# A four-layer attention decoder: another order of one head's TensorE steps, query and table buffers moved, one logits bank per block

## The chip, the core and the metric

The kernel runs on one core of a Trainium2 chip. The time is device microseconds (us) of one execution. The kernel before takes 1056.14 us, the median of 3 runs (1054.42 to 1060.06). The profiled execution took 1054.78 us; its trace spans 1053.0 us, at a mean granted TensorE clock of 0.992.

## The reference

Four layers work on a sequence of 512 tokens of width 1024. Layer i uses mixer i mod 3: multi-head latent attention (MLA), sliding-window attention (SWA), forgetting attention (FoX), and MLA again. Each has 16 heads with values of 64 columns, and all is in fp32:

```
for i in range(4):
    y = mixer[i % 3](x)                      # (o * silu(gate)) @ w_out
    x = layernorm(8 ** 0.25 * x + y)
# one head o:  s = scale * q @ k.T (+ bias) ; causal mask ; p = softmax(s) ; o = p @ v
# MLA: q and k have 64 plain columns and 32 rotary ones, from low-rank projections with an RMS norm
# SWA: a query sees 128 keys at most; ALiBi bias, a sink per head, 4 key/value heads for 16 query heads
# FoX: bias cum[q] - cum[k], cum = running sum of log_sigmoid(f)
```

## The kernel before, in words

Tensors lie with 128 rows on the partitions. A matrix product in fp32 is made of fp32r products: each operand is split into a high part (a cast on ACT) and a low part (a subtraction on VectorE or GpSimd), and high x high, high x low and low x high are summed in PSUM, so a product takes three passes. The logits of SWA and FoX take two passes, because high and low halves of a 64-column key are stacked in the 128 rows.

**Weights.** One list holds all weight units in the order of their use. A unit is loaded by SP's DMA queue into a raw tile of 512 KB (`_raw`, L254, pool `p_wr`, tag "wr", 3 buffers), cast on ACT (L289), and its low part is subtracted in halves of 512 columns on GpSimd (L293; on VectorE for the output weights "O"). `W()` splits up to three units ahead of the one in use. When the split of unit k is issued, the load of unit k+2 is issued behind it.

**PSUM.** Eight banks: three for projections ("pp", `bank()`), two for logits ("ss"), two for transposes ("pt"), one for a head's output ("oo").

**A head.** Queries come in four blocks of 128. The step S(qb) makes the logits of block qb (TensorE, `mm`, L305), and VectorE adds the bias or mask and takes the row extreme (L844 in MLA, L905 in SWA, L1024 and L1026 in FoX). After the fourth block the softmax tail runs: exponentials on ACT (L420), a reciprocal on VectorE (L426), scaling of blocks 0 to 2 on GpSimd (L431) and of block 3 on ACT (L429). The step T transposes the probabilities through the identity matrix (L479 for MLA and FoX, three groups of 4, 3 and 3 blocks; L926 for SWA, two groups of 4 and 3). Each group fills one "pt" bank, which is emptied by a cast on ACT (L465) and a subtraction on VectorE (L309) into a tile "PT". The step PV multiplies with the values (TensorE), ACT and VectorE empty the bank (L503, L504), and for every second head GpSimd multiplies with the gate (L511).

**Order on TensorE.** In the loop over heads the order of TensorE's instructions is the program order (a manual schedule); the other engines' orders are planned by a scheduler. The steps of iteration h come from `slots`:

```
sn = st["s_fn"](h + 1, st) if h + 1 < H else []
pv = [lambda: self.attn_pv(h - 1, st)] if h else []
return sn[:2] + pv + sn[2:] + st["t_fn"](h, st)
```

That is S0 S1 of head h+1, PV of head h-1, S2 S3 of head h+1, and all transposes of head h (T0 T1 T2, or T0 T1 in SWA). Between the steps `heads` spreads filler: the projections of later heads. `PAIRS` lists for each pair of heads which ones: K, Q, V and G are key, query, value and gate projections, R the rotary query projection for four heads. The last pair is filled with steps of the output projection (`out_part`, 49 steps of three matmuls, L305, named "po" or "pp"), `TAIL` and `EXTRA` of them; `finish` makes the rest and the layer norm after a hand-written list (`FINISH`: f is so many output steps, k, m the closing ones, r the residual on VectorE, L545, s, t, a, b the norm), in which VectorE's order is the program's too.

**MLA's start.** `PRO` gives how many gate and value steps (g and d) are put between the transposes of the compressed queries, the rotary projection, the query projection and the key projection. Behind the key projection and nine further gate steps the head loop begins, and the remaining value steps fill its first blocks.

**Rotary part of MLA's queries.** The projection R ends in a bank; VectorE multiplies it with a table of cosines and sines (L811), which a DMA brings from memory (L808, input "cs", 512 KB) into a tile of pool `p_rt`, tag "tq". The product stays in that tile, ACT casts it and GpSimd subtracts (L813, L814) into "rq", and for each head two DMAs (L831, 128 KB each) copy its rows into the query tile of that head, pool `p_qk`, tag "qk", which holds the plain part (ACT L825, VectorE L826).

## Time and profile before

| | us |
|---|---|
| median of 3 runs (lowest, highest) | 1056.14 (1054.42, 1060.06) |
| profiled execution, its span | 1054.78, 1053.0 |
| PE busy (5416 matmuls) | 993.0 (94% of the span) |
| ACT, VectorE (DVE), GpSimd (POOL) busy | 623.0, 610.3, 508.8 |
| head loops of layers 0, 1, 2, 3 | 61.4 to 240.9, 307.9 to 454.8, 546.0 to 755.4, 835.1 to 1013.0 |

The four head loops together take 713.7 us of the span; the rest is the layers' projections ahead of the loops, the ends of the output projections and the layer norms. In the page of the profile a busy share is a mean over the span. In the rows further down a row of a wait reads: engine, output tile and line of the waiting instruction, then engine, tile and line of what ended the wait, then the idle time in us, the number of waits and the longest. A row of the order of instructions reads: start in us, duration in us, engine, line, operation, output from input, partitions x elements, count, and in brackets the idle time ahead of it with what ended it. A row of windows reads: window, its length, then busy time and count of each engine, the granted clock (1.00 is full), the DMA share and the GB/s. "SPq" is SP's DMA queue.

### The profile page before, as it was taken

Reading aid. Unit: us, or ns where it says so; the run is one execution under the profiler, and the core shown is the slowest. Engines: PE = TensorE matmul, PEld = TensorE weight load, DVE = VectorE, ACT = ScalarE, POOL = GpSimd, SP = SyncE. Lnnn points to the kernel's source line nnn. Section 1 sums busy time; section 2 is a strip of 40 time slices with the busy share of each in tenths; the row PEclk is TensorE's granted clock in tenths of the full one; section 3 lists DMA queues with packets and bytes.
Section 4 is the critical chain, followed back from the end, with each engine's and each line's share of the span. In section 5 each row is a group of like instructions: output and inputs, shape, how many; then the busy total and the mean of one; then the engine's idle time right before and its main releaser. Section 6 shows DMA issues by size and latency. Waiting matters only on the chain.

```text
span 1053.0 us, 15941 instructions
## 1 busy us (share of the span) xinstructions
PE 993.0 (94%) x5416; PEld 843.7 (80%) x5416; DVE 610.3 (58%) x1501; ACT 623.0 (59%) x1350; POOL 508.8 (48%) x572
## 2 busy tenths in 40 slices
PE   8999898999999999999999999999999998999895
PEld 8978787778888887788988888887879787777784
DVE  2566666853735656819334555566366567567717
ACT  4477877753346777723456666666344588677712
POOL 5755555333245664413456666642175556553303
PEclk9999999999999999999999999999999999999998
DMA  6452322452542122414342343335252533223412
GB/s 222 133 152 93 91 69 80 126 170 77 204 120 81 61 81 81 147 56 160 106 145 82 108 113 101 110 119 167 74 164 74 178 103 90 74 71 101 130 41 81
DMA packets 37218, 116.77 MB, mean 111 GB/s; under 512 B 5376, under 2 KB 5632, under 8 KB 36880
## 3 DMA queue, kind: packets, MB, share of 16 engines
q1 hardware_dynamic: 37136, 115.75, 35.7%
q8 instruction: 43, 0.70, 0.3%
q14 instruction: 39, 0.32, 0.1%
HBM read 92.62 MB, written 8.42 MB: 96 GB/s over the span
## 4 chain that ended last, share of the span: by engine, by line
PE 43%; ACT 3%; DVE 3%; issue 2%; DMA 1%; POOL 1%; SPq 0%; DVEq 0%; POOLq 0%; ACTq 0%
PE pp L305 29%; PE ss L305 4%; PE po L305 4%; PE oo L305 3%; PE ptt L479 3%; DMA wr<-in_w 1%; ACT w L289 1%; ACT P L420 1%; POOL r L609 1%; PE pxt L356 1%; DVE PT L309 1%; DVE r L593 0%; ACT PT L465 0%; DVE w L293 0%; DMA q<-rq 0%
## 5 line engine op out<-in xcount | busy, mean ns | idle before, releaser
L305 PE MATMUL pp<-xT,w 128*128 128x512 f32 (+1 forms) x1440 | 376.9, 394 | 0.0
L293 POOL TENSOR_TENSOR w<-wr,w 128x512 fp32r<-128x512 f32 x202 | 241.8, 1222 | 204.9 <-ACT w L289 125.5
L305 PEld LDWEIGHTS pp<-xT,w 128*128 128x128 f32 x1440 | 249.3, 190 | 36.9
L431 POOL TENSOR_TENSOR P<-P,rs 128x256 f32<-128x256 f32 (+2 forms) x192 | 113.3, 618 | 130.7 <-DVE rs L426 129.7
L420 ACT ACTIVATE P<-P,m 128x256 f32<-128x256 f32 (+3 forms) x256 | 137.7, 539 | 63.9 <-DVE m L844 32.6
L289 ACT CAST w<-wr 128x1024 fp32r<-128x1024 f32 (+4 forms) x117 | 115.3, 990 | 101.3 <-PE pp L305 47.1
L309 DVE TENSOR_TENSOR PT<-ptt,PT 128x384 fp32r<-128x384 f32 (+1 forms) x176 | 104.1, 601 | 65.5 <-ACT PT L465 65.2
L305 PE MATMUL pp<-w,xT 128*128 128x256 f32 (+2 forms) x768 | 112.8, 300 | 2.3 <-ACT xT L360 1.9
L305 PEld LDWEIGHTS pp<-w,xT 128*128 128x128 f32 x768 | 105.4, 191 | 3.8 <-ACT xT L360 2.4
L465 ACT CAST PT<-ptt 128x384 fp32r<-128x384 f32 (+1 forms) x176 | 88.3, 513 | 26.9 <-PE ptt L479 21.6
L479 PE MATMUL ptt<-ident,P 128*128 128x128 f32 x480 | 77.1, 275 | 23.6 <-DVE PT L309 21.6
L479 PEld LDWEIGHTS ptt<-ident,P 128*128 128x128 f32 x480 | 58.5, 140 | 49.7 <-DVE PT L309 32.9
L305 PEld LDWEIGHTS oo<-PT,v 128*128 128x128 f32 x512 | 81.8, 188 | 12.6 <-DVE PT L309 2.9
L305 PE MATMUL pp<-cT,w 128*128 128x512 f32 x312 | 90.3, 404 | 0.0
L305 PE MATMUL ss<-kt,q 128*128 128x128 f32 (+3 forms) x384 | 82.6, 323 | 6.5 <-ACT kt L797 2.7
L305 PE MATMUL oo<-PT,v 128*128 128x256 f32 (+3 forms) x512 | 85.7, 307 | 1.4 <-DVE PT L309 1.4
L504 DVE TENSOR_TENSOR o<-oo,o 64x512 f32<-64x512 f32 x64 | 44.0, 688 | 68.0 <-ACT o L503 67.7
L305 PEld LDWEIGHTS ss<-kt,q 128*128 128x128 f32 x384 | 65.2, 188 | 19.8 <-ACT kt L797 3.6
L305 PE MATMUL pp<-w,oT 128*128 128x512 f32 x288 | 79.3, 402 | 0.0
L844 DVE CUSTOM_DVE_ANT_0 P<-ss,mask 128x128 f32<-128x128 f32 (+3 forms) x128 | 61.6, 487 | 23.8 <-PE ss L305 21.5
L305 PE MATMUL po<-wo,oT 128*128 128x512 f32 x288 | 70.7, 395 | 0.0
L511 POOL TENSOR_TENSOR o<-o,g 128x512 f32<-128x512 f32 x28 | 36.3, 1295 | 61.8 <-DVE o L504 61.8
(120 smaller groups left out, 1433.2 us busy)
## 6 DMA issues: line engine op xcount, KB each, us to landing
wr<-in_w SPq DMA_DIRECT2D x110, 512.0 KB, 3.4
q<-rq SPq DMA_DIRECT2D x64, 128.0 KB, 2.4
xd<-r SPq DMA_DIRECT2D x12, 512.0 KB, 2.9
r<-xd SPq DMA_DIRECT2D x12, 512.0 KB, 3.9
wr<-in_w SPq DMA_DIRECT2D x16, 336.0 KB, 3.4
kd<-kd SPq DMA_DIRECT2D x20, 256.0 KB, 4.3
tq<-in_cs SPq DMA_DIRECT2D x8, 512.0 KB, 3.9
cb<-cd SPq DMA_DIRECT2D x16, 256.0 KB, 3.4
```

What stands on the lines that cost most here:

```text
L289: nc.scalar.copy(w[0][:, :c], r[:, :c])
L293: eng.tensor_tensor(w[1][:, a:b], r[:, a:b], w[0][:, a:b].bitcast(F32), op=ALU.subtract)
L305: self.nc.tensor.matmul(out, l, r, start=start, stop=stop)
L309: (eng or self.nc.vector).tensor_tensor(out, src, hi.bitcast(F32), op=ALU.subtract)
L356: nc.tensor.transpose(v, xt[:, c:c + 128], self.ident[:])
L420: nc.scalar.activation(v, v, AF.Exp, bias=m[:, c:c + 1], scale=-1.0, accum_out=sums[:, c:c + 1])
L431: nc.gpsimd.tensor_tensor(v, v, rs[:, c:c + 1].to_broadcast([128, v.shape[1]]), op=ALU.mult)
L465: nc.scalar.copy(pt[:, 0, :n], ps[:, :n])
L479: nc.tensor.transpose(ps[:, c:c + 128], Ps[qb][:, kb * 128:(kb + 1) * 128], self.ident[:])
L504: nc.vector.tensor_tensor(o[a, :], o_ps[a, :], o[a, :], op=ALU.add)
L511: eng.tensor_tensor(o[:], o[:], g[:], op=ALU.mult)
L844: nc.vector.tensor_tensor_reduce(out=P[:, :n], in0=ps[:, :n], in1=self.mask[:, S - n:], scale=1.0, scalar=3e38, op0=ALU.add, op1=ALU.min, ...
```

## The change

The step order of an iteration is new (`iteration`). Per head of MLA and FoX it is now: T0 of head h, S2 of head h+1, T1, S3 of head h+1, T2, then S0 and S1 of head h+2, then PV of head h itself. S0 and S1 of a head are thus issued one iteration earlier than before, PV of a head right in its own iteration. In SWA (two transposes) it is S2 S3 of head h+1, T0 T1, S0 S1 of head h+2, PV; round the loop these are the same neighbours as before. `GROUPS` takes the place of `PAIRS` and `EXTRA`: the same projections are dealt to groups of iterations counted in a rotation fitting the new order, "+n" stands for n output steps, and the first group (count 0) holds head 0's four logits, S0 and S1 of head 1 and the remaining value steps. `TAIL` has fewer entries, one for each step of the last two iterations.

The third query buffer: for heads with h mod 3 = 2 the query tile comes from pool `p_rt`, tag "tq", the buffer in which the table was before. The table's tile now comes from pool `p_wr`, tag "wr", the three raw-weight buffers.

In SWA each of the four logits blocks gets an "ss" bank tile of its own, where two blocks shared one.

In the last layer `FINISH` takes 16 free output steps instead of 22 ahead of the closing ones (the "+7" and the new tail hold another number too), and `PRO` puts four value steps beside the key projection in both MLA layers, where it had two and none.

No product is added or left out.

```diff
@@ -40,16 +40,16 @@
     'f91 k0 f99 k1 r0 s0 k2 m1 r1 t0 s1 r2 s2 k3 m4 a0 b0 x0 h3 t2 t1 a1 b1 m3 i3 s3 x1 a2 b2 t3 a3 x2 b3 x3',
     'f38 k0 f99 k1 k3 r0 s0 r1 t0 k2 s1 a0 b0 a1 h3 t1 m3 x0 r2 b1 m5 s2 i3 s3 a2 t2 b2 x1 t3 a3 b3 x2 x3',
     'f33 k3 f99 k0 k1 r0 s0 r1 t0 m4 a0 k2 s1 b0 t1 a1 x0 b1 m4 r2 h3 s2 a2 x1 t2 i3 b2 s3 t3 a3 b3 x2 x3',
-    'f22 k0 k1 k2 f99 r0 r1 s0 s1 t0 m1 z0 k3 r2 t1 s2 a1 m5 b1 m2 t2 h3 a2 b2 i3 s3 a3 t3 b3',
+    'f16 k0 k1 k2 f99 r0 r1 s0 s1 t0 m1 z0 k3 r2 t1 s2 a1 m5 b1 m2 t2 h3 a2 b2 i3 s3 a3 t3 b3',
 )
-PRO = ((2, 1, 2, 2), (2, 1, 19, 0))
+PRO = ((2, 1, 2, 4), (2, 1, 19, 4))
 PRE = 4
 
 TAIL = (
-    (1, 1, 1, 1, 1, 1, 2, 3, 4, 1, 2, 3),
-    (1, 1, 1, 1, 2, 2, 4, 4, 1, 4),
-    (1, 1, 1, 1, 1, 1, 3, 4, 4, 1, 2, 3),
-    (1, 1, 1, 1, 1, 1, 2, 3, 4, 1, 2, 3),
+    (1, 1, 1, 2, 3, 4, 1, 2, 4),
+    (1, 2, 2, 3, 4, 2, 4),
+    (1, 1, 1, 2, 3, 4, 1, 2, 4),
+    (1, 1, 1, 2, 3, 4, 1, 2, 4),
 )
 
 
@@ -63,14 +63,14 @@
 
 
 
-PAIRS = (
-    ("K1 Q1 R1 G2", "K2 Q2 V1", "K3 Q3 R2 G3", "K4 Q4 G4", "K5 Q5 R3 G5", "K6 Q6 G6", "K7 Q7 G7"),
-    ("G0 Q2", "G1 Q3", "G2 Q4", "G3 Q5", "G4 Q6", "G5 Q7", "G6 G7"),
-    ("V2 Q2 K2", "G2 Q3 K3", "G3 Q4 K4", "V3 Q5 K5", "G4 Q6 K6", "G5 Q7 K7", "G6 G7"),
+
+GROUPS = (
+    ((0, "K1 Q1"), (1, "V1"), (2, "R1 K2 Q2 G2"), (2, "K3 Q3 G3"), (2, "R2 K4 Q4 G4"), (2, "K5 Q5 G5"), (2, "R3 K6 Q6 G6"),
+     (2, "K7 Q7 G7"), (1, "+7")),
+    ((0, "G0"), (2, "Q2 G1"), (2, "Q3 G2"), (2, "Q4 G3"), (2, "Q5 G4"), (2, "Q6 G5"), (2, "Q7 G6"), (2, "G7 +8")),
+    ((0, "G2"), (2, "V2 Q2 K2"), (2, "G3 Q3 K3"), (2, "G4 Q4 K4"), (2, "V3 Q5 K5"), (2, "G5 Q6 K6"), (2, "G6 Q7 K7"), (2, "G7 +16")),
 )
-STREAM = tuple(jobs(" ".join(k)) for k in PAIRS)
-
-EXTRA = (3, 0, 8, 3)
+STREAM = tuple(tuple(j for _, k in g for j in jobs(k) if j[0] != "+") for g in GROUPS)
 FIRST = (jobs("G0 G1 K0 R0 Q0 V0"), jobs("Q0 Q1"), jobs("K0 Q0 G0 K1 Q1 G1"))
 
 def layer_units(kind):
@@ -610,54 +610,62 @@
         nc.sync.dma_start(self.t["out"][tb * 128:(tb + 1) * 128, :], r[:])
 
 
-    def job_cols(self, kind, n, a):
-
+    def job(self, layer, st, make, n, a):
+
+        kind = layer % 3
+        if n == "+":
+            return islice(st["order"], a), a * 3 * 512
         if kind == 0 and n in "KQR":
-            return (6 if n == "K" else 9) * 512
-        return 96 * 256 if n == "V" and kind else 24 * 512
-
-    def slots(self, layer, st, h):
-
-        sn = st["s_fn"](h + 1, st) if h + 1 < H else []
-        pv = [lambda: self.attn_pv(h - 1, st)] if h else []
-        return sn[:2] + pv + sn[2:] + st["t_fn"](h, st)
-
-    def run_heads(self, layer, st, make, pre=iter(()), npre=3):
+            return make[n](a), (6 if n == "K" else 9) * 512
+        return make[n](a), 96 * 256 if n == "V" and kind else 24 * 512
+
+    def iteration(self, layer, st, h):
+
+
+        sn = st["sn"].pop(h + 1, [])
+        tn = st["t_fn"](h, st)
+        if h + 2 < H:
+            st["sn"][h + 2] = st["s_fn"](h + 2, st)
+        new = st["sn"].get(h + 2, [])
+        mixed = [f for f in chain.from_iterable(zip_longest(tn, sn[2:])) if f] if len(tn) > 2 else sn[2:] + tn
+        return mixed + new[:2] + [lambda: self.attn_pv(h, st)]
+
+    def run_heads(self, layer, st, make, pre=iter(()), npre=0):
 
         with self.tc.manual_schedule(engines={mybir.EngineType.PE}):
             self.heads(layer, st, make, pre, npre)
 
     def heads(self, layer, st, make, pre, npre):
-        kind = layer % 3
         st["order"] = self.out_part(layer, st)
-        st["P"], st["PT"], st["oT"] = {}, {}, []
-        for f in st["s_fn"](0, st):
-            f()
-            self.run(islice(pre, npre))
-        self.run(pre)
-        for p in range(NP - 1):
-            todo = jobs(PAIRS[kind][p])
-            total = sum(self.job_cols(kind, n, a) for n, a in todo)
-            gen = chain.from_iterable(make[n](a) for n, a in todo)
-            if p == NP - 2:
-                gen = chain(gen, islice(st["order"], EXTRA[layer]))
-                total += EXTRA[layer] * 3 * 512
-            done = i = 0
-            for h in (2 * p, 2 * p + 1):
-                steps = self.slots(layer, st, h)
-                for f in steps:
+        st["P"], st["PT"], st["oT"], st["sn"] = {}, {}, [], {1: st["s_fn"](1, st)}
+        h = 0
+        for count, todo in GROUPS[layer % 3]:
+            work = [self.job(layer, st, make, n, a) for n, a in jobs(todo)]
+            gen, total = chain.from_iterable(g for g, _ in work), sum(c for _, c in work)
+            if count:
+                its = [self.iteration(layer, st, h + i) for i in range(count)]
+            else:
+                gen, total = chain(pre, gen), total + npre * 3 * 512
+                its = [st["s_fn"](0, st) + st["sn"][1][:2]]
+            done = 0
+            for k, steps in enumerate(its):
+                for i, f in enumerate(steps):
                     f()
-                    i += 1
-                    while done + 768 < total * i / (2 * len(steps)):
+                    while done + 768 < total * (k + (i + 1) / len(steps)) / len(its):
                         c = self.cols
                         if next(gen, self) is self:
                             break
                         done += self.cols - c
             self.run(gen)
-        self.cq_done(layer)
-        steps = self.slots(layer, st, H - 2) + self.slots(layer, st, H - 1) + [lambda: self.attn_pv(H - 1, st)]
-        for f, n in zip_longest(steps, TAIL[layer], fillvalue=0):
+            h += count
+            if layer % 3 == 0 and h == H - 3:
+                self.cq_done(layer)
+        steps = self.iteration(layer, st, H - 2)
+        last = self.iteration(layer, st, H - 1)
+        for i, (f, n) in enumerate(zip_longest(steps + last, TAIL[layer], fillvalue=0)):
             f()
+            if i == 3:
+                self.cq_done(layer)
             self.run(islice(st["order"], n))
         self.finish(layer, st)
 
@@ -804,7 +812,7 @@
         def rproj(g):
 
             def done(ps):
-                t = self.p_rt.tile([128, 2, S], F32, tag="tq", name=self.nm("tq"))
+                t = self.p_wr.tile([128, 2, S], F32, tag="wr", name=self.nm("tq"))
                 nc.sync.dma_start(t[:], self.t["cs"])
                 r = self.p_rt.tile([128, 2, 2, S], F32R, tag="rq", name=self.nm("rq"))
                 for i in range(2):
@@ -821,7 +829,8 @@
                 for odd in range(2):
                     h = 2 * p + odd
                     own, r0 = (slice(64, 128), 0) if odd else (slice(0, 64), 64)
-                    t = self.p_qk.tile([128, 2, S], F32R, tag="qk", name=self.nm("q"))
+                    pool, tag = (self.p_rt, "tq") if h % 3 == 2 else (self.p_qk, "qk")
+                    t = pool.tile([128, 2, S], F32R, tag=tag, name=self.nm("q"))
                     nc.scalar.activation(t[own, 0, :], ps[own, :], AF.Copy, scale=C_MLA)
                     nc.vector.scalar_tensor_tensor(t[own, 1, :], in0=ps[own, :], scalar=C_MLA, in1=t[own, 0, :].bitcast(F32),
                                                    op0=ALU.mult, op1=ALU.subtract)
@@ -895,14 +904,13 @@
                     if h % 2 == 1:
                         qt.pop(h // 2)
                     env["P"] = []
-                if qb % 2 == 0:
-                    env["ps"] = self.ps_s.tile([128, 2, 256], F32, tag="ss", name=self.nm("ss"))
-                ps, m, pss = env["ps"], env["m"], env["passes"]
+                ps = self.ps_s.tile([128, 512], F32, tag="ss", name=self.nm("ss"))
+                m, pss = env["m"], env["passes"]
                 P = self.ptile(qb)
                 k0, n = (0, 128) if qb == 0 else ((qb - 1) * 128, 256)
                 for a, (q, k) in enumerate(pss):
-                    self.mm(ps[:, qb % 2, 256 - n:], q[:, qb * 128:(qb + 1) * 128], k[:, k0:k0 + n], a == 0, a == len(pss) - 1)
-                nc.vector.tensor_tensor_reduce(out=P[:, :n], in0=ps[:, qb % 2, 256 - n:], in1=ali[h // NP][:, h % NP, 256 - n:],
+                    self.mm(ps[:, :n], q[:, qb * 128:(qb + 1) * 128], k[:, k0:k0 + n], a == 0, a == len(pss) - 1)
+                nc.vector.tensor_tensor_reduce(out=P[:, :n], in0=ps[:, :n], in1=ali[h // NP][:, h % NP, 256 - n:],
                                                scale=1.0, scalar=3e38, op0=ALU.add, op1=ALU.min,
                                                accum_out=m[:, qb:qb + 1])
                 env["P"].append((P[:, :n], qb))
```

## The prediction

> **What bounds the kernel now.** I read the page's busy shares first, then busy time by stage, then what TensorE waits for stage by stage, and last the order of instructions in one head. The four windows below are the four layers' head loops (latent, sliding window, forgetting, latent), from the first logits to the last output of a head.
>
> ```profile
> PE 993.0 (94%) x5416; PEld 843.7 (80%) x5416; DVE 610.3 (58%) x1501; ACT 623.0 (59%) x1350; POOL 508.8 (48%) x572
> ...
> core 0: us, PE busy (x) PEld busy (x) DVE busy (x) ACT busy (x) POOL busy (x), PEclk, DMA share, GB/s
> 61.40:240.90 179.50, 166.07 (x881) 137.79 (x882) 116.85 (x284) 132.55 (x295) 86.54 (x96) 1.00 0.37 110
> 307.90:454.80 146.90, 140.06 (x769) 115.50 (x768) 92.96 (x261) 100.35 (x257) 72.66 (x87) 1.00 0.28 89
> 546.00:755.40 209.40, 206.50 (x1135) 175.72 (x1134) 118.45 (x358) 130.62 (x280) 112.96 (x114) 0.99 0.38 112
> 835.10:1013.00 177.90, 164.53 (x877) 137.04 (x878) 116.11 (x283) 129.78 (x292) 81.46 (x92) 1.00 0.34 96
> ```
>
> TensorE bounds all of it. Window less PE busy is the idle time: 13.4, 6.8, 2.9 and 13.4 us, 36.5 in all. No other engine is near its limit (ACT at most 74%). What ends that idle time, over the whole span:
>
> ```profile
> PE ptt L479 <- DVE PT L309: 21.6, 19, 2.0
> PE ss L305 <- DVE m L905: 6.6, 12, 1.5
> ...
> PE ss L305 <- ACT q L825: 1.7, 4, 0.4
> PE ss L305 <- DVE q L826: 1.6, 6, 0.3
> ```
>
> The large one is a transpose group waiting for VectorE to empty a transposed tile (two banks, three groups per head); the second is sliding-window logits waiting for the reduction of the neighbouring block in the same bank. By window, the waits number 18, 12, 3 and 18. Each costs a little more than its idle time:
>
> ```profile
> 145.65 1.14 PE L305 MATMUL pp<-xT,w 128*128 128x512 f32 x4
> 146.62 0.69 PE L305 MATMUL ss<-kt,q 128*128 128x384 f32 x3
> ...
> 349.01 1.09 PE L305 MATMUL pp<-xT,w 128*128 128x512 f32 x4
> 350.42 0.51 PE L305 MATMUL ss<-kd,q 128*128 128x256 f32 x2 [0.31 <-DVE m L905]
> ```
>
> Four projections take 0.97 start to start without a wait and 1.41 with an idle of 0.31, so 0.13 more per wait: 51 x 0.13 = 6.6. About 43 us can be won in the loops.
>
> **The change part by part.** No matrix work is added or removed; instructions change places, buffers and dependences.
>
> *Transposes alternating with logits (latent and forgetting layers).* Here is one stalled group:
>
> ```profile
> 169.57 0.60 PE L479 MATMUL ptt<-ident,P 128*128 128x128 f32 x4
> 171.36 0.58 ACT L465 CAST PT<-ptt 128x512 fp32r<-128x512 f32 x1
> 171.98 0.69 DVE L309 TENSOR_TENSOR PT<-ptt,PT 128x512 fp32r<-128x512 f32 x1 [1.37 <-ACT PT L465]
> 172.73 0.55 PE L479 MATMUL ptt<-ident,P 128*128 128x128 f32 x3 [1.29 <-DVE PT L309]
> ```
>
> The first group's bank is empty 3.1 us after it starts (169.57 to 172.67); the third group wants it after two filler gaps. With a logits block and a filler gap more between each two, that distance doubles, so these waits go. What is late next is the softmax. Today nine steps lie between a head's last logits and its first transposes; afterwards five filler gaps, the third transposes of the head before, two logits and an output. The chain it must cover:
>
> ```profile
> 167.96 0.85 PE L305 MATMUL ss<-kt,q 128*128 128x512 f32 x3
> 170.75 1.75 POOL L431 TENSOR_TENSOR P<-P,rs 128x128 f32<-128x128 f32 x3 [3.19 <-DVE rs L426]
> ...
> 178.61 0.85 PE L305 MATMUL ss<-kt,q 128*128 128x512 f32 x3
> 184.38 1.75 POOL L431 TENSOR_TENSOR P<-P,rs 128x128 f32<-128x128 f32 x3
> ```
>
> From the logits' end (168.81, 179.46) to GpSimd's last scaling it takes 3.7 us in a good head and 6.7 in a bad one. A head with 24 filler matmuls has three per gap (0.70: 149.12's four take 1.01, 152.00's three 0.74), so 5 x 0.70 + 2.2 for the fixed steps = 5.7 us; with 19.5, about 5.0. Between no wait (3.7) and 1.7 (6.7 against 5.0) I take 0.3 per head, output waits included, because two of the old evacuations no longer stand in the chain: 28 latent heads x 0.3 = 8.4. The first head has three gaps only: 0.3 twice. In the last heads VectorE also splits the output weights; 2 us a layer stay.
>
> *Third query buffer.* The query waits above (3.3 us) go; a new projection finds its buffer free. SP, the DMA queue, no longer stands before query loads for the old buffer (first row, nearly 62 us of queue time).
>
> ```profile
> SPq L831 <- PE ss L305: 61.9, 20, 8.0
> SPq L808 <- POOL rq L309: 26.4, 4, 6.8
> ```
>
> *The rotary table moves into a weight buffer.* This is the price of that buffer. Today the table (cs) has its own buffer and is loaded long before use. Afterwards it takes a raw-weight buffer, in turn. Those three are never idle: a weight load starts the moment GpSimd ends the split of the unit three earlier. The loads at 62.81 and 832.47 show it:
>
> ```profile
> 42.36 0.33 SPq L808 DMA_DIRECT2D tq<-in_cs  x1
> ...
> 62.81 0.33 SPq L254 DMA_DIRECT2D wr<-in_w  x1
> 832.47 0.50 SPq L254 DMA_DIRECT2D wr<-in_w  x1
> ...
> 60.26 2.52 POOL L293 TENSOR_TENSOR w<-wr,w 128x512 fp32r<-128x512 f32 x2 [1.95 <-ACT kt L781]
> 829.90 2.54 POOL L293 TENSOR_TENSOR w<-wr,w 128x512 fp32r<-128x512 f32 x2
> ...
> 54.05 1.29 DVE L811 TENSOR_TENSOR tq<-pp,tq 128x512 f32<-128x512 f32 x2 [1.51 <-PE pp L305]
> 57.08 3.03 SPq L831 DMA_DIRECT2D q<-rq  x4
> 58.95 1.64 PE L305 MATMUL pp<-cT,w 128*128 128x512 f32 x6
> 831.50 1.64 PE L305 MATMUL pp<-cT,w 128*128 128x512 f32 x6
> ...
> DMA to landing us min/median/max: 3.2/3.9/5.6
> ```
>
> When the first rotary projection finishes, the weight loads already asked for are ahead of the table, and the buffer it gets is the one now filled at 62.81 (832.47 in the last layer). It lands 3.9 us later (the row above is of the table's tile). From the table's product to the first queries' rotary rows took 54.05 to 60.6 (the second of the four loads, 58.33 and 2.3 to land), 6.55 us. So the first logits start at 62.8 + 3.9 + 6.55 = 73.3 and 832.5 + 3.9 + 6.55 = 842.9. TensorE has until then the key projection (six at 0.23 from 58.95 and 831.50, to 60.3 and 832.9) and what PRO puts behind it: 12 value matmuls and 4 of a gate at 0.23 each (3.7 us, to 64.0) and 12 (2.8, to 835.7). The new waits are 9.3 and 7.2 us. Bounds: nothing, if the buffer comes free early, and some 2 us more in the first layer, where the pending product also holds a projection bank. I take the middle reading, since the rows are this stage's own. The waits that PRO was to cover (0.8, 1.9 and 0.5, with 0.4 for their ends, 3.6) go with it. For the six later tables the same rule gives landing 8 to 9 us after the projection starts, its bank wanted 9.7 after; VectorE and the query loads in SP stand behind it: 0 to 2 each, 0.35 taken, 2 in all.
>
> *The clock.* A long wait costs again afterwards:
>
> ```profile
> 714.50:718.50 4.00, 2.08 (x12) 1.43 (x11) 3.07 (x6) 2.48 (x6) 1.95 (x4) 1.00 1.02 302
> 718.60:722.00 3.40, 3.40 (x12) 2.82 (x11) 1.61 (x2) 2.67 (x4) 1.28 (x1) 0.50 0.40 155
> 722.80:726.20 3.40, 3.40 (x19) 3.00 (x18) 3.36 (x10) 2.16 (x6) 0.00 (x0) 1.00 0.52 167
> ```
>
> After the 1.9 us wait of the forgetting layer 12 matmuls ran at half clock where 19 follow at full: 3.4 x 7/19 = 1.25 us, won back when that wait goes, paid once for each new long wait (2.5). [...]
>
> *A bank per logits block.* The third logits' reader no longer blocks the fourth: 6.8 + 12 x 0.13 = 8.4 goes, 1 us stays at the first head, whose softmax now has three gaps. *Two logits ahead, groups and tails:* same steps in another rotation; 1.5 us of new waits in the forgetting layer, whose keys now have some 7 us instead of a head to arrive. *End:* FINISH closes after 42 instead of 46 output steps:
>
> ```profile
> 1028.93 0.69 DVE L545 SCALAR_TENSOR_TENSOR r<-r,pp 128x512 f32<-128x512 f32 x1 [12.53 <-PE pp L305]
> 1035.57 5.01 PE L305 MATMUL pp<-wo,oT 128*128 128x512 f32 x21
> 1045.57 0.67 DVE L545 SCALAR_TENSOR_TENSOR r<-r,pp 128x512 f32<-128x512 f32 x1
> ```
>
> VectorE's chain starts four steps of three matmuls (2.8 us) earlier; TensorE ends at 1040.6, well ahead of 1045.57, so all 2.8 show.
>
> *The sum*, against the profiled 1054.8 us (span 1053.0, 1.8 around it): latent loops -(26.8 + 36 x 0.13 - 3.6) = -27.9, new waits +8.4 + 0.6 + 4 + 2 = +15, net -12.9; sliding window -7.4; forgetting -(2.9 + 0.4 + 1.25) + 1.5 = -3.1; end -2.8; prologues +9.3 + 7.2 + 2.5 - 3.6 = +15.4. Together -10.8: 1044.0. The median of the runs is 1.4 above the profiled one, so I say 1045.
>
> **The rivals.** *The table is not late* (a weight buffer is free when it is asked for). For it: only three buffers for two pending units and one in work, so one may be spare between bursts; against: the loads above start at the end of a split. The prologues then give -3.6 instead of +15.4: 1026.
> *The softmax becomes the bound* (slower). Place: the first transposes of each latent head. At 1.2 us per head instead of 0.3, 28 x 0.9 = 25 more: 1070. No gain is left from about 0.7 a head. For it: the 6.7 us head; against: the 3.7 us head, and fewer evacuations in the way.
> *The alternation doesn't free the transposes*, because VectorE, which now has a reduction before each evacuation, is as late as before: the latent loops stay, the prologues' cost is partly in the same idle time, and the other parts win a little: 1056.
>
> **How the numbers follow.** Forecast 0.52, table not late 0.25, no effect 0.12, softmax bound 0.11. About 0.5% (5.3 us) is what a measurement of this kernel can tell from no change: faster ends at 1050.9, slower begins at 1061.4. The forecast's own range is 1034 to 1056 (3.7 or 6.7 us softmax, 0 to 2 us more at the prologue): three quarters of it counts as faster, the rest as same. Faster 0.39 + 0.25 + 0.02 = 0.66, same 0.13 + 0.08 = 0.21, slower 0.13. The range 1016 to 1060 leaves out most of the slow rival and the edge of the fast one, some 0.18.
>
> **What would show it.** Right: waits of transposes on VectorE's evacuation down from 21.6 us to a few; no wait on L905; table loads (rotary projection) issued just after a weight split; one idle stretch of 7 to 10 us ahead of each latent layer's first logits, ended by a query load or the products behind it, with a dip of the clock; new short waits of transposes on GpSimd's or ScalarE's scaling; VectorE's last residual near 2.8 us sooner against TensorE's end. The prediction is wrong if the table load is issued well before the split ends (then 1026), or if TensorE's waits on the scaling exceed 20 us.

## The result: 1.3% slower, and the profile after

The changed kernel takes 1071.28 us (median of 4 runs, 1067.26 to 1074.27), against 1056.68 us of the kernel before in the same measurement: ratio 1.0133 (95% interval 1.0089 to 1.0177). The profiled execution has a span of 1072.5 us and a mean granted clock of 0.978 (before: 1053.0 and 0.992). Forecast were 1045 us and a range of 1016 to 1060.

First the page's busy shares of the changed kernel:

```profile
PE 1008.9 (94%) x5416; PEld 860.0 (80%) x5416; DVE 607.7 (57%) x1501; ACT 620.6 (58%) x1350; POOL 509.2 (47%) x572
```

Then its busy time by window, which are the four head loops (columns as before):

```profile
76.70:244.80 168.10, 161.65 (x871) 136.28 (x872) 110.94 (x276) 127.12 (x288) 84.24 (x94) 1.00 0.38 115
310.50:464.50 154.00, 146.18 (x784) 120.94 (x783) 94.76 (x261) 100.04 (x256) 74.50 (x87) 0.99 0.27 85
552.30:778.40 226.10, 213.80 (x1147) 182.18 (x1146) 118.12 (x358) 130.48 (x279) 112.26 (x114) 0.97 0.36 104
864.80:1036.40 171.60, 165.88 (x871) 140.03 (x872) 110.27 (x275) 125.62 (x285) 79.82 (x90) 0.97 0.33 98
```

The same 5416 matmuls keep TensorE busy 15.9 us longer than before (993.0). Nothing was added; they ran at a lower mean clock. The clock column says where: 0.97 in the forgetting and the last latent loop. What TensorE waits for over the whole span has changed its names altogether:

```profile
PE ptt L479 <- POOL P L431: 15.3, 21, 4.0
PE oo L305 <- DVE PT L309: 6.6, 16, 0.8
PE ss L305 <- DMA q<-rq: 6.1, 3, 3.0
PE pp L305 <- DVE q L835: 4.6, 2, 2.5
...
PE pp L305 <- DVE kt L309: 3.0, 1, 3.0
PE ss L305 <- DMA kd<-kd: 2.5, 1, 2.5
PE pp L305 <- DVE tq L819: 2.0, 1, 2.0
...
PE ptt L479 <- DVE PT L309: 0.6, 2, 0.3
```

The last row was 21.6 us: the alternation did what it says. All rows together went from 47 to 53 us. By stage (us; "moved" is the work that the new groups put into another stage: matmuls of 512 columns, counted at 0.23, the time from one start to the next in this trace, as in the row of 377.91 below, where four take 0.93; "rest" is the change without it):

| stage | before | after | change | moved | rest |
|---|---|---|---|---|---|
| to layer 0's first logits | 61.4 | 76.7 | +15.4 | +3.7 | +11.7 |
| latent loop, layer 0 | 179.5 | 168.1 | -11.4 | -2.3 | -9.1 |
| sliding-window loop | 146.9 | 154.0 | +7.2 | +3.5 | +3.7 |
| forgetting loop | 209.3 | 226.1 | +16.8 | +2.8 | +14.0 |
| to layer 3's first logits | 79.7 | 86.4 | +6.6 | 0.0 | +6.6 |
| latent loop, layer 3 | 177.9 | 171.6 | -6.3 | -1.4 | -4.9 |
| end | 40.0 | 36.1 | -3.9 | -1.4 | -2.5 |
| the two stages left | 158.3 | 153.5 | -4.8 | -4.8 | 0.0 |

So the latent loops and the end won about what was forecast, and three places lost: the starts of the latent layers (foreseen), the sliding-window loop and the forgetting loop (not foreseen).

**The starts.** The order of SP, GpSimd, VectorE and TensorE ahead of layer 0's first logits, changed kernel:

```profile
64.35 2.49 POOL L293 TENSOR_TENSOR w<-wr,w 128x512 fp32r<-128x512 f32 x2 [11.66 <-issue]
66.86 0.33 SPq L816 DMA_DIRECT2D tq<-in_cs  x1
70.31 1.29 DVE L819 TENSOR_TENSOR tq<-pp,tq 128x512 f32<-128x512 f32 x2 [2.75 <-DMA tq<-in_cs]
...
63.05 1.62 PE L305 MATMUL pp<-cT,w 128*128 128x512 f32 x6 [2.49 <-DVE q L835]
67.71 1.94 PE L305 MATMUL pp<-w,cT 128*128 128x512 f32 x6 [3.04 <-DVE kt L309]
71.65 2.93 PE L305 MATMUL pp<-w,cT 128*128 128x512 f32 x6 [2.00 <-DVE tq L819]
```

The split ends at 66.84, the table load is issued at 66.86 (42.36 before), and its product is made 3.4 us later. The bank of the rotary projection is held until then, so TensorE runs out of banks three times before the first logits at 76.74.

**The sliding-window loop.** One head of the changed kernel on TensorE:

```profile
376.19 0.49 PE L934 MATMUL ptt<-ident,P 128*128 128x128 f32 x3
376.43 1.18 PE L305 MATMUL pp<-xT,w 128*128 128x512 f32 x4
377.45 0.62 PE L305 MATMUL ss<-kd,q 128*128 128x128 f32 x4
377.91 1.08 PE L305 MATMUL pp<-xT,w 128*128 128x512 f32 x4
378.84 0.62 PE L305 MATMUL oo<-PT,v 128*128 128x256 f32 x3
379.91 0.80 PE L305 MATMUL oo<-PT,v 128*128 128x256 f32 x5 [0.46 <-DVE PT L309]
```

The four "ss" matmuls are two logits blocks with no filler between them. The output starts 2.65 us after the last transposes and waits for their evacuation, that is, until ACT and VectorE have emptied their bank.

**The forgetting loop.** GpSimd and TensorE at the first transposes of its first head, then of head 13:

```profile
560.89 1.27 POOL L1023 TENSOR_TENSOR cb<-cb,mask 128x512 f32<-128x512 f32 x1 [5.71 <-DMA cb<-cd]
...
563.34 1.75 POOL L431 TENSOR_TENSOR P<-P,rs 128x128 f32<-128x128 f32 x3
563.79 1.04 PE L479 MATMUL ptt<-ident,P 128*128 128x128 f32 x2 [4.05 <-POOL P L431]
...
741.30 1.26 POOL L1023 TENSOR_TENSOR cb<-cb,mask 128x512 f32<-128x512 f32 x1 [8.55 <-DMA cb<-cd]
742.52 1.75 POOL L431 TENSOR_TENSOR P<-P,rs 128x128 f32<-128x128 f32 x3
742.97 0.33 PE L479 MATMUL ptt<-ident,P 128*128 128x128 f32 x1 [2.39 <-POOL P L431]
```

The reciprocal that the first head's scaling needs had been ready since 559.63. GpSimd stood at the bias of a later head, for whose load it waited, and the scaling was queued behind it. At the first head TensorE waits 4.4 us for it in all, at head 13 3.1; the other heads have 0.9 together. The time between the end of a head's fourth logits and its first transposes, in which TensorE does other steps, is called its cover here. Without the wait the first head has 3.2 us of cover (8.2 in the kernel before), and most heads have 7.4 to 8.7 (11.1 to 16.6 before). In the kernel before GpSimd stands at such a load too, ahead of the scaling of head 12, which ends 8.5 us after that head's fourth logits; there 12.9 us of cover hide it:

```profile
704.13 1.28 POOL L1015 TENSOR_TENSOR cb<-cb,mask 128x512 f32<-128x512 f32 x1 [8.93 <-DMA cb<-cd]
705.37 2.66 POOL L431 TENSOR_TENSOR P<-P,rs 128x128 f32<-128x128 f32 x3
```

**The clock.** Windows of 3.41 us of the changed kernel, each followed by the one after it:

```profile
434.08:437.49 3.41, 2.09 (x11) 1.57 (x12) 2.37 (x9) 3.41 (x9) 2.53 (x4) 1.00 0.46 154
437.49:440.90 3.41, 3.41 (x12) 2.83 (x11) 3.41 (x8) 1.43 (x3) 0.12 (x1) 0.50 0.45 125
...
560.37:563.78 3.41, 0.00 (x0) 0.00 (x0) 0.69 (x1) 0.96 (x2) 2.89 (x4) 1.00 0.00 0
563.78:570.61 6.83, 6.42 (x27) 5.84 (x28) 1.34 (x4) 0.59 (x1) 2.54 (x3) 0.50 0.23 77
```

Each stretch at half clock (0.50) follows a window in which TensorE stood for 1.3 to 3.4 us, and is one or two windows long. Not every such window has one behind it: that of 62.02, with 1.8 us, has none. The half-clock stretches of this trace start whole multiples of 3.413 us apart: the one at 437.49 is 108 of them behind the first, at 68.85, and the one at 1007.52 275. Up to the end of the last head loop there are twelve windows at half clock; the kernel before has one after its first 12 us.

### The profile page after: what moved, and what is told of

The parts are those of the page before. It is cut to its first block, busy times and chain, and to the rows that moved or that the text cites. A ratio compares the mean times of both kernels' runs of the same rounds, so it can differ in the third digit from the quotient of the medians.

```text
span 1072.5 us, 15953 instructions
## 1 busy us (share of the span) xinstructions
PE 1008.9 (94%) x5416; PEld 860.0 (80%) x5416; DVE 607.7 (57%) x1501; ACT 620.6 (58%) x1350; POOL 509.2 (47%) x572
## 5 line engine op out<-in xcount | busy, mean ns | idle before, releaser
L305 PE MATMUL pp<-w,xT 128*128 128x256 f32 (+2 forms) x768 | 116.3, 306 | 2.0 <-ACT xT L360 1.8
L305 PEld LDWEIGHTS pp<-w,xT 128*128 128x128 f32 x768 | 108.8, 196 | 3.8 <-ACT xT L360 2.5
L479 PE MATMUL ptt<-ident,P 128*128 128x128 f32 x480 | 82.8, 278 | 16.4 <-POOL P L431 15.3
L305 PE MATMUL oo<-PT,v 128*128 128x256 f32 (+3 forms) x512 | 89.5, 310 | 8.6 <-DVE PT L309 6.6
L479 PEld LDWEIGHTS ptt<-ident,P 128*128 128x128 f32 x480 | 60.8, 141 | 39.8 <-POOL P L431 21.7
L305 PE MATMUL pp<-w,oT 128*128 128x512 f32 x288 | 85.5, 421 | 0.6 <-POOL oT L309 0.6
L305 PEld LDWEIGHTS po<-wo,oT 128*128 128x128 f32 x288 | 53.2, 188 | 11.3
```

The source lines that it names most:

```text
L305: self.nc.tensor.matmul(out, l, r, start=start, stop=stop)
L479: nc.tensor.transpose(ps[:, c:c + 128], Ps[qb][:, kb * 128:(kb + 1) * 128], self.ident[:])
```

## The experiments

Times are compared by their ratio to the kernel before of the same measurement, turned into us at its 1056.7; the changed kernel is then 1070.7.

**e1: the table in its own buffer, two query buffers.**

```diff
-                t = self.p_wr.tile([128, 2, S], F32, tag="wr", ...)
+                t = self.p_rt.tile([128, 2, S], F32, tag="tq", ...)
...
-                    pool, tag = (self.p_rt, "tq") if h % 3 == 2 else (self.p_qk, "qk")
+                    t = self.p_qk.tile([128, 2, S], F32R, tag="qk", ...)
```

> The changed kernel with the third query buffer undone: the table is in its own buffer again, queries have two. Theory A (the loss has three places: the table late at the start of the latent layers, the forgetting layer's transposes waiting for GpSimd, sliding-window outputs waiting for the evacuation; each long wait is followed by a stretch at half clock): before the head loops the excess over the matmuls' own pace grew by 11.8 us in layer 0 and 5.5 in layer 3, about 1.7 of the latter not from the table; 15 to 16 go, some 3 come back as query waits: 1058 to 1060. Theory B (the new order of the steps is what costs; the late table is mostly hidden by work that had to wait anyway): 1066 to 1073.

Measured 1052.06 us, ratio 0.9959 (0.9938 to 0.9980), 18.4 us faster than the change. Layer 0's first logits come at 61.6, as before. It is theory A, and more than it said: no query wait came back. With two query buffers no wait of logits on a query stands in its list, so the buffer that was bought with the table wins nothing in the new order.

**e2: the forgetting layer's transposes together.**

```diff
-        mixed = [...] if len(tn) > 2 else sn[2:] + tn
+        mixed = [...] if layer % 3 == 0 else sn[2:] + tn
```

> The changed kernel with the transposes of the forgetting layer together again, behind both logits (the old neighbours); all else as changed. Theory A: the forgetting layer's loop has 14 us more over its matmuls' own pace, 11.1 of it at transposes that wait for the scaling and the half clock behind; with them together the first transposes come two steps later and it goes: 1057 to 1061. Theory C (the layer is slower because two logits stand ahead and keys and bias rows arrive late, whatever the transposes do): no more than 5 us, 1066 to 1072.

Measured 1057.63 us, ratio 1.0013 (0.9997 to 1.0029), 12.7 us faster than the change. The loop is 212.0 us (226.1), as theory A has it. What TensorE waited for in that loop, first in the changed kernel:

```profile
PE ptt L479 <- POOL P L431: 8.4, 7, 4.0
PE ss L305 <- DMA kd<-kd: 2.5, 1, 2.5
```

and in e2:

```profile
PE ptt L479 <- DVE PT L309: 2.1, 2, 1.9
PE ptt L479 <- POOL P L431: 0.7, 2, 0.5
```

All waits in the loop fall from 12.3 to 3.7 us; half-clock windows in it from four to one, up to 1.71 us each. 8.6 + 5.1 = 13.7 of the 14.1 us. GpSimd still stands 5.28 us at a bias ahead of the first scaling, but the transposes now come late enough to wait only 0.7 us for it. The four profiles in which nothing in this loop was touched (the change, e1, e3, e5) have 226.1, 225.0, 224.3 and 221.9, so the loss is 10 to 14 us: they differ by up to 1.9 us of waits and one half-clock window.

**e3: two sliding-window blocks in one bank again** (the three lines of the diff on `ps` undone).

> The changed kernel with two sliding-window logits blocks in one bank again. Theory A: TensorE then waits at the fourth logits, as before, and no longer at the output; the layer is 3 to 4 us faster: 1067 to 1068. Theory D (the bank is worth the 7 us that were forecast, and another step of the layer, its groups or order, costs 11): slower by 7, 1078. If the layer is set by one loop of engines whatever the bank, the time stays 1071 and the wait only changes its name.

Measured 1085.35 us, ratio 1.0273 (1.0241 to 1.0306): 14.8 us slower than the change. Theory A is wrong. The bank is worth twice the 7 us that were forecast, in this order: the first two logits stand next to each other, and in one bank the second waits for the reader of the first.

```profile
393.28 0.33 PE L305 MATMUL ss<-kd,q 128*128 128x128 f32 x2
394.99 0.50 PE L305 MATMUL ss<-kd,q 128*128 128x256 f32 x2 [1.38 <-DVE m L914]
```

So something else in this layer cost some 18 us against the kernel before, of which the bank gave 14 back. That it was the place of the filler was the next theory.

**e4: useless transposes in TensorE's long waits.**

```diff
-            self.run(kproj(0), islice(v0, d))
+            if layer == 0:
+                self.idle_fill(20)
+            self.run(kproj(0))
+            self.idle_fill(28 if layer == 0 else 20)
+            self.run(islice(v0, 2))
+            if layer == 0:
+                self.idle_fill(18)
+            self.run(islice(v0, d - 2))
             g(9)
+            if layer:
+                self.idle_fill(28)
...
+            if layer == 2 and not count:
+                self.idle_fill(40)
```

> The changed kernel with useless transposes of the identity put into TensorE's long waits: 66 in the start of layer 0, 48 in that of layer 3, 40 ahead of the first transposes of the forgetting layer, 0.084 us each, shorter than the wait that they fill. Nothing becomes ready sooner. Theory E (the clock is granted for stretches of 3.41 us by how busy TensorE was in the one before, so that filling a wait saves the half clock behind it): seven half-clock stretches, 12 us at half speed of which some lies over waits that stay, go: 1062 to 1066. Theory F (the waits themselves are the cost and the low clock after them falls on work that has slack): 1071 to 1073.

Measured 1068.29 us, ratio 1.0120 (1.0093 to 1.0148): between the theories, and no difference from the change that the ratios can show. The traces differ by 6.2 us (1066.3 against 1072.5). The half clock went at every filled place (mean clock 0.988, in the change 0.978); the transposes took 0.109 us each, not 0.084 (20 in 2.35 us, 28 in 3.22), and filled the waits. Ahead of layer 0's logits that gave nothing (76.6 against 76.7):

```profile
71.50 1.65 PE L305 MATMUL pp<-w,cT 128*128 128x512 f32 x6 [0.38 <-DVE tq L827]
...
76.62 0.52 PE L305 MATMUL ss<-kt,q 128*128 128x128 f32 x3 [2.56 <-DMA q<-rq]
```

TensorE got through its work sooner and waited for the query rows instead: there the table sets the time, and theory F holds. In the forgetting loop, 221.9 us, the gain is no more than the spread of unfilled profiles (221.9 to 226.1). Layer 3's loop, 169.2 where the change, e2, e3 and e5 have 170.8 to 171.6, won some 2 us. Of the 5 to 9 us that theory E promised little is left; where the clock costs wasn't settled by this run.

**e5: the empty filler gap moved.** Twelve groups of four filler matmuls go into the fourteen gaps of two sliding-window heads. The rule puts the next group of 2048 columns into a gap when the columns done, and 768 more, are fewer than the share due by then, 1755 a gap. After four groups 8192 + 768 = 8960 is above 5 x 1755 = 8775, so the fifth gap of each head stays empty. In the order before that was behind S3, in the rotated one it is behind S0, between the transposes and the output.

```diff
-                    while done + 768 < total * ...:
+                    while done + (1500 if layer % 3 == 1 else 768) < total * ...:
```

> The changed kernel with one number of the filler rule changed for the sliding-window layer: twelve filler groups go into fourteen gaps of two heads, and the two gaps that stay empty lie behind the fourth logits, as in the kernel before, and no longer behind the first logits (between the transposes and the output). Theory G (the loss of the layer is the missing filler group ahead of the output, 0.93 us of cover, and not the bank): the output's wait of 0.8 per head goes, and the logits' wait stays away: 8 to 11 us faster than the changed kernel, 1060 to 1063. Theory H (with a bank per block the exponentials are ready sooner and ACT takes them before the cast of the transposed tile, so the output waits wherever the filler stands): 1069 to 1072.

Measured 1056.77 us, ratio 1.0024 (1.0006 to 1.0042): 11.5 us faster than the change. Theory G, and more than its 8 to 11. One head of it:

```profile
380.29 0.49 PE L934 MATMUL ptt<-ident,P 128*128 128x128 f32 x3
380.54 1.17 PE L305 MATMUL pp<-xT,w 128*128 128x512 f32 x4
381.55 0.33 PE L305 MATMUL ss<-kd,q 128*128 128x128 f32 x2
381.72 1.14 PE L305 MATMUL pp<-xT,w 128*128 128x512 f32 x4
382.69 0.40 PE L305 MATMUL ss<-kd,q 128*128 128x256 f32 x2
382.93 1.09 PE L305 MATMUL pp<-xT,w 128*128 128x512 f32 x4
383.86 1.04 PE L305 MATMUL oo<-PT,v 128*128 128x256 f32 x8
```

From the transposes to the output it is 3.57 us now (2.65), and the output doesn't wait. The loop is 141.1 us (154.0).

**e6: the kernel before with a bank per block**, nothing else.

> The kernel before with a logits bank per block in the sliding-window layer, nothing else. Theory G: the term that was forecast, 7 us faster than before: 1049 to 1051. Theory H: the wait moves from the logits to the output: 1055 to 1059.

Measured 1052.09 us, ratio 0.9967 (0.9954 to 0.9979): 3.5 us faster than before, between the two theories. The loop falls from 146.9 to 143.4; the wait on the logits' reader goes from 6.6 to 0.8 us, and the output waits for the evacuation, 3.5 us in six places. The bank alone is worth half of what was forecast. In e5, with another order of the filler jobs, the output's wait does not appear; why it does in e6 wasn't tried.

**e7: the three together** (the edits of e1, e2 and e5).

> The changed kernel with three things put right together: the table in its own buffer (two query buffers), the forgetting layer's transposes together, the empty filler gaps of the sliding-window layer behind the fourth logits. The three losses lie in different layers: if they add up, 1071.3 - 19.2 - 13.6 - 8 to 11 = 1028 to 1031 under theory G, 1038 under theory H. If they were one loss seen three times (the clock, or a rhythm that each edit shifts), the sum is not reached: 1043 or more.

Measured 1025.78 us, ratio 0.9716 (0.9694 to 0.9738): 44.0 us faster than the change, where 18.4 + 12.7 + 11.5 make 42.6. The losses add up, to a little more than expected (1028 to 1031). Its sliding-window and forgetting loops, at full clock nearly all the time:

```profile
299.40:440.40 141.00, 139.46 (x784) 119.08 (x783) 95.71 (x261) 100.93 (x256) 75.55 (x87) 1.00 0.28 93
528.20:740.70 212.50, 208.42 (x1147) 178.56 (x1147) 119.59 (x358) 130.17 (x279) 114.00 (x114) 0.99 0.36 111
```

**e8: e7 with the latent transposes together as well** (`mixed = sn[2:] + tn` for every layer).

> The kernel of the run before this one with the transposes of the latent layers together again as well: it keeps the two logits ahead, the groups, tails and closing of the last layer. The forecast's term for the alternation in the latent loops was 12.9 us net, so 13 slower than that run (11 to 15). If the gain of the latent loops comes from the rotation and the tails alone: within 3 of it.

Measured 1039.45 us, ratio 0.9846 (0.9822 to 0.9870): 13.7 us slower than e7. The alternation in the latent layers is worth what the forecast said (12.9). Transposes wait 23.9 us for VectorE again, 2.3 in e7.

**e9: e7 with the third query buffer and the table in a weight buffer, asked for early.**

```diff
             if (t, tb) == (1, NT - 1):
+                self._raw(self.index[(layer, "QK", 0, 0)])
+                cs0 = self.p_wr.tile([128, 2, S], F32, tag="wr", ...)
+                nc.sync.dma_start(cs0[:], self.t["cs"])
                 self.hold = len(self.units)
...
+                if g == 0:
+                    t = cs0
```

> The kernel of e7 with the third query buffer and the table in a weight buffer again, as in the change, but the first table of each latent layer is asked for before the last projection block of the compressed queries, behind the load of the first query and key weights, instead of when its product is wanted. Theory A (only the late request costs): 1024 to 1030, as e7, the first logits near 62 us and no half clock before them; equal to e7 means also that the third query buffer is worth nothing. Theory J (three raw buffers are too few for weights and a table, whenever it is asked for): the weight splits of the start come late, 1033 or more.

Measured 1030.81 us, ratio 0.9747 (0.9711 to 0.9782): some 3 us slower than e7, between the theories. The first logits come at 64.0, after a wait of 2.97 us for the query rows and with half clock behind it (mean clock of the profile 0.985, in e7 0.993). Most of the start's loss was the late request; the arrangement with the third query buffer still wins nothing over e7.

**e10: e7 with one wait filled.** 20 useless transposes ahead of the third transposes of head 12 of the forgetting layer.

> The kernel of e7 with 20 useless transposes of 0.084 us ahead of the one long wait of its forgetting layer (1.97 us, third transposes of head 12), which has 3.41 us of half clock behind it. Theory E (filling the wait saves the half clock): the layer's loop 1.0 to 1.7 us shorter than e7's 212.45 and no half clock in it. Theory F: the same loop time. The total can't tell the two apart.

Measured 1026.56 us, ratio 0.9719 (0.9686 to 0.9752), the total like e7's. The loop is 210.8 us and has no half-clock window. The same loop with the wait unfilled and the half clock behind it took 212.0 to 212.5 (e2, e7, e8, e9), and 211.1 in e12, whose profile has the wait but no half clock behind it. Why it was spared is not known: in the stretch with the wait TensorE is busy 1.59 us in e12 and in e9, and only e9 has half clock after it. Theory E: in this loop, where TensorE sets the time, a half-clock window cost 1.0 to 1.6 us, by one profile of each kernel; half of 3.41 is 1.71.

**e11: e7 with the forgetting layer alternating, its bias added on VectorE.**

```diff
-            nc.gpsimd.tensor_tensor(v(1), v(0), self.mask...)
+            nc.vector.tensor_tensor(v(1), v(0), self.mask...)
```

> The kernel of e7 with the forgetting layer's transposes alternating, as in the change, and its bias plus mask added on VectorE instead of GpSimd. With GpSimd this arrangement would take 1025.8 + 13.6 = 1039. Theory K (the scaling is late because GpSimd stands before it at the bias of the next head, waiting for its load): the waits of the transposes on the scaling fall from 11 us to 3 or less, 1030 to 1034. Theory L (alternating leaves too few steps between logits and transposes whoever adds the bias): 1037 to 1041.

Measured 1035.33 us, ratio 0.9808 (0.9760 to 0.9855), between the theories, and 9.7 us slower than e7. The wait on the scaling in this loop falls from 8.4 to 3.8 us, but 3.8 us of wait at the first head stay. VectorE now stands at the same load, with the reciprocal behind it (GpSimd, at a weight split, adds the last 0.7 us):

```profile
535.67 1.21 DVE L1022 TENSOR_TENSOR cb<-cb,mask 128x512 f32<-128x512 f32 x1 [1.34 <-DMA cb<-cd]
...
537.06 0.17 DVE L426 RECIPROCAL rs<-sm 128x4 f32<-128x4 f32 x1
```

And outputs wait for VectorE's evacuation (3.4 us). The loop is 221.1 us, 8.6 longer than with the transposes together.

**e12: e7 with the third logits ahead of the first transposes in the latent layers** (`zip_longest(sn[2:], tn)`).

> The kernel of e7 with another alternation in the latent layers: third logits, first transposes, fourth logits, second, third transposes. The first transposes come one logits block and one filler gap later (1.2 us more for the scaling), the third still 1.4 us later against the first than when all were together. If the scaling is what is left there (8.5 + 1.6 us of waits in 21 places, and 0.13 behind each): 1015 to 1019. If the third transposes then wait for the evacuation: 1023 to 1028.

Measured 1022.90 us, ratio 0.9679 (0.9651 to 0.9706): the fastest of the series, by some 4 us against e7, at the edge of the 1023 to 1028 that were expected with waits for the evacuation. In the profiles the two latent loops win 2.5 us of it; another 1.4 lie in the forgetting loop, whose code is the same, but which got no half-clock window. The waits on the scaling fall from 8.5 to 0.7 us. Not all of it is won: in each latent layer one output waits 3.4 us for the evacuation, with half clock behind it.

**e13: e7 with the forgetting layer alternating and a third bias buffer.**

```diff
+        cb3 = self.p_rt.tile([128, 2, S], F32, tag="tq", ...)
...
+        def cbuf(h):
+            return cb3 if h % 3 == 2 and h < 14 else cb2[:, (h % 3) % 2] if h < 14 else cb2[:, h % 2]
```

> The kernel of e7 with the forgetting layer's transposes alternating, as in the change, and a third buffer for the bias rows (in the tile that the table uses in the latent layers, heads 2, 5, 8 and 11), so that the load for two heads ahead needs not wait for the last logits of the head in work. The bias is added on GpSimd, as in the change. Theory K2 (the alternation costs here because an engine stands in front of the scaling at a bias that can't be loaded earlier): the wait of 4 us at the first head and the waits on the scaling go, the loop falls from 222 to 226 us to 213 to 215, 1027 to 1030. Theory L (the alternation leaves too few steps for the softmax of this layer, whatever the bias): the loop stays at 219 or more, 1033 to 1039.

Measured 1038.91 us, ratio 0.9842 (0.9823 to 0.9861), loop 224.8: the buffer won nothing, as theory L has it. That does not settle it for theory L, because the scheduler used the buffer to load one head further ahead (three bias loads before the loop, two in the change), and GpSimd again stood at a load with the scaling behind it:

```profile
537.37 1.26 POOL L1026 TENSOR_TENSOR cb<-cb,mask 128x512 f32<-128x512 f32 x1 [5.66 <-DMA cb<-cd]
...
539.82 1.75 POOL L431 TENSOR_TENSOR P<-P,rs 128x128 f32<-128x128 f32 x3
```

**e14: e13 with the third logits ahead of the first transposes in both kinds of layer.**

> The kernel of e13 with the alternation of e12 (third logits ahead of the first transposes) in the latent and the forgetting layers. Under K2 nothing of the forgetting layer is left to wait for the scaling and its loop is no longer than with the transposes together (211 to 212): 1022 to 1024, as e12. Under L the logits block ahead adds one filler gap of 1 to 2 us to the cover and the loop comes to 212 to 214 from 219 or more: 1023 to 1026, so e13 tells the two apart and this run says whether the alternation can be had in this layer at all.

Measured 1025.36 us, ratio 0.9721 (0.9705 to 0.9737). The forgetting loop is 213.7 us, as theory L has it (212 to 214): 2.5 us more cover (9.96 in seven heads that have 7.42 in e13) hides the scaling in all heads but the first and head 13. It is still no better than the transposes together (212.5). In this layer, with longer filler gaps, they hardly waited in the kernel before (1.9 us), so there was nothing to win.

What stays open: why GpSimd's planned order puts the bias of a later head ahead of the scaling of the one in work, and how much of the loss the order of GpSimd alone would win back. An order with the two exchanged wasn't tried.

## Why the prediction was wrong, point by point

The forecast put the sum at -10.8 us; the traces differ by +19.5. Without the moved work, 17.1 us of the miss lie in the forgetting layer, 11.1 in the sliding-window layer and 2.9 in the starts; the rest came out within about 1 us each. So the two layers for which the forecast had no rival made most of the miss.

- *What bounds the kernel; the evacuation as the large wait.* Right: 21.6 us of waits became 0.6.
- *Alternation in the latent loops, -12.9.* Right: -9.1 and -4.9 in the stages, 13.7 by e8. That e8 meets the net figure so closely is in part luck, since the net held other terms too (query waits, the first and last heads). The new wait on the scaling was put at 0.3 per head; in the latent loops it was 15.3 - 8.4 = 6.9 us in 28 heads, 0.25 each.
- *Third query buffer, 3.3 us of query waits.* The waits went, but not by the buffer: e1, e7 and e8 have two buffers and none of these waits. What in the new order removed them was not tried.
- *The table late, +15.4 in the starts.* The mechanism was right to its release: 66.86 is the end of a split, and so is 853.86 in layer 3. In layer 0 the split itself came 4 us later than in the kernel before, which the forecast had not. +11.7 and +6.6 measured, 18.4 by e1.
- *The clock, 1.25 us for each new long wait, two of them.* The mechanism was seen, the count was wrong: twelve half-clock windows. The price of 1.25 was right where TensorE sets the time (1.0 to 1.6 by e10). The step that failed is "paid once for each new long wait": in the trace half clock comes in windows of 3.41 us, and it also follows one with less idle time than the 1.9 us of that row (434.08 above, 1.3 us).
- *A bank per logits block, -7.4; measured +3.7.* The step that failed is "same steps in another rotation", by which the new order was to cost nothing in this layer. The order of the steps round the loop is the same, but the filler rule leaves out a fixed gap counted from the start of the list, and the rotation moved that gap from behind S3 to the 3.6 us that hid the evacuation. Two lines of arithmetic on the rule would have shown it. The bank by itself was mis-sized too: 3.5 us in the old order (e6), where outputs began to wait. With the gap moved back the layer won more than forecast (e5: 141.1 us with 3.5 us more work in it, against 146.9).
- *The forgetting layer, -3.1; measured +14.0.* Worst of all (10 to 14 lost), and a term that was put at nothing: the sum has new waits on the scaling for the 28 latent heads and none here. The cover of the softmax was worked out for the latent heads only. In seven heads of this layer it fell from 12.9 us to 7.4, at the first head from 8.2 to 3.2, and the scaling ends up to 8.6 us after the logits (15.6 at head 13). That it can be late was already in the trace of before: in the heads whose fourth logits end at 584.81 and 609.04 it ended 6.6 us after them, and in the head of 699.53 8.5 us after them, behind the bias load shown above, with 12.9 us of cover to hide it. The late arrival of keys was priced (1.5 us; 2.5 measured).
- *End, -2.8.* Right: from TensorE's last matmul to the end it takes 9.9 us instead of 12.4.
- *The rivals.* The time of the softmax rival (1070) was hit by luck, but not its place: it was put at the latent heads, which won. Neither sign of being wrong showed (the table is issued at the end of the split, and the waits on the scaling come to 15.3 us): no sign had been set for new waits in the sliding-window layer.

## What to carry to other kernels

When a list of steps is rotated, the neighbours stay but everything that is counted along the list moves: work out which gap gets no filler, and what that gap was hiding. A change that is right for one kind of layer has to be priced again for each other kind, with the cover that each has now: three losses of 11 to 18 us turned a gain of 30 into a loss of 14. And ask when a rotating pool gives its buffer: the one that the table took came by the pool's turn, not by when it was asked for (its load was issued at 66.86, when the split before it had ended at 66.84); the cheapest test is to undo one part at a time.

## What the runs showed of the hardware

In the traces of both kernels half clock comes in stretches of 3.41 us, up to the end of the last head loop one or two at a time, and their starts are whole multiples of 3.413 us apart (in the kernel before the one at 718.56 is 208 of them behind the first, at 8.59). In the changed kernel TensorE stood for 1.3 to 3.4 us in the stretch ahead of each. The length of the idle time alone doesn't tell it: the one of 434.08, with 1.3 us of idle time, has half clock behind it, but in the kernel before the one of 213.39, with 1.9 us, has none:

```profile
213.39:216.80 3.41, 1.52 (x9) 0.91 (x7) 3.41 (x8) 3.39 (x9) 0.37 (x2) 1.00 0.83 299
216.80:220.21 3.41, 3.30 (x19) 2.90 (x20) 2.35 (x6) 1.72 (x3) 2.36 (x3) 1.00 0.76 228
```

Half clock cost nothing where another engine set the time (e4, layer 0: first logits at 76.6 us without it, 76.7 with it) and 1.0 to 1.6 us a window where TensorE did (e10).
